# Split in-projection weights written to DRAM by the first token block and read back by the other two

## The chip, the cores and the metric

The kernel runs on one core of one Trainium2 chip. The metric is device time in microseconds of one execution. Below, PE is the matmul engine (TensorE) and PEld its weight loads, DVE is VectorE, ACT ScalarE, POOL GpSimd, and SP the engine whose queue issues all of this kernel's DMAs.

## The reference, cut to what matters

One layer of a hybrid encoder: a projection, a gated MLP mixer beside a Mamba-2 state-space mixer, an output projection, a layer norm, and a squared-ReLU feed-forward. The change touches the projection alone.

```python
def mixer(x, ssm_state, conv_state, offset, w_in, ...):
    proj = jnp.einsum('bld,de->ble', x, w_in)          # 1024 -> 4624 columns
    u, v, z, xbc, dt = ...                             # slices of proj
    y_g, v_rows = gmlp_mix(u, v, ...)
    xbc, new_conv = causal_conv(xbc, conv_state, conv_w, conv_b)
    y, new_ssm = ssd_scan(xs, dtp, a, bm, cm, ssm_state)
    y_s = gated_rms_norm(y, z, ssd_norm_g)
    out = jnp.einsum('ble,ed->bld', jnp.concatenate([y_g, y_s], axis=-1), w_out)
```

There are 2048 prompt rows and 8 x 16 sample rows, so 17 chunks of 128 rows, all in float32.

## The kernel before, in words

The program has four stages: the mixer (projection, state-space tasks, gated-MLP tasks), the output projection, and the two feed-forward products. Only the mixer is touched; its last projection product runs at about 1085 us of the profiled span.

**Blocks and units.** The 17 chunks are taken in three token blocks of 6, 6 and 5 chunks (`BLOCKS`). Each block walks 18 units of the projection in the order of the list `order` (z0, x4, x5, x0, ... v3); a unit is 256 output columns (272 for z0, which also holds dt). So every unit's weights are used three times, once per block.

**Products in three passes.** A float32 value is split into a high part (rounded to the type fp32r) and a low part (the rest). `split` does this with one cast on ACT (line 55) and one subtraction on DVE (line 56). A product is made from three of the four pairs of parts (`PASSES`), with both parts of both operands in fp32r. `fl_matmul` (line 217, tile `psfl`) serves the x and u units, `tl_matmul` (line 225, tile `pstl`) the z and v units; each unit has 96 to 144 matmuls.

**Weights.** `load_w` allocates a tile `w` for both parts (128 partitions x 2 parts x 8 k-slices x 272) from a pool of two buffers. For each half of k it loads 512 KB of float32 into a staging tile `ws` (the pool `st` of three buffers, shared with `xs_in`, the staging of x) on line 120, and splits it into `w`. At the start of unit i the code asks for the weights of unit i+1, so their buffer is the one that unit i-1 has just left. This is done in every block: 18 x 3 units, two halves each.

**Mixing tasks.** After each unit one task of a list runs: `ssd(b, j, g)`, a state-space task of one chunk and one half of the heads, or `gmlp(b, j)`. An ssd task loads `xs`, `bt`, `bc`, `e` (from `at`) and `z` from DRAM, where the units left them. ACT and DVE turn `e` into decay factors (lines 425 to 432), and PE multiplies them (`yd`, line 439). At the end it writes `ys` (line 504). The buffers of `xs` and `e` are two deep, so a task's loads wait for the task two before it. The gmlp tasks of a block run in the first five units of the next block: they load `v` and `ug` (from `u`) and multiply with `wt` (tile `sg`, line 533).

**What sets the order.** The program is written in the order above, and a scheduler then places each instruction on its engine's list by a timeline of its own. On the chip every engine, SP included, goes through its list in order: an instruction whose wait isn't over holds everything behind it. DMAs take eight semaphores in turn, so the ninth can only be issued when the first has landed.

Of the kernel before, what the change touches and what calls it, by code (L numbers as in the profile page):

```python
# [7 lines left out]
F32 = mybir.dt.float32  # L8
# [6 lines left out]
P = 128  # L15
D = 1024
KD = D // P
# [33 lines left out]
def trunk_kernel(ctx: ExitStack, tc: tile.TileContext, A, O):  # L51
# [30 lines left out]

    right = ExitStack()
    tail = mixer_heads(tc, right, psA, A, O, dr, small, stage, ident, select, rsqrt, split, yg_d, ys_d)
    sums = Sums(nc, A, dr, stage, x1_d)
    out_proj(tc, right, psA, tail, A, dr, small, stage, rsqrt, split, yg_d, ys_d, x1_d, sums.during_out_proj)
# [4 lines left out]
def mixer_heads(ctx, tc, right, psA, A, O, dr, small, sp, ident, select, rsqrt, split, yg_d, ys_d):  # L91
    nc = tc.nc
# [14 lines left out]

    order = ["z0", "x4", "x5", "x0", "x1", "z1", "x2", "x3", "z2", "z3", "u0", "u1", "u2", "u3", "v0", "v1", "v2", "v3"]

    def load_w(u):  # L110
        w = wp.tile([P, 2, KD, 272], F32R, name="w", tag="w")
        for q in range(2):
            load_w_half(w, u, q)
        return w

    def load_w_half(w, u, q):
        n = 272 if u == "z0" else 256
        src = A["w_z0"] if u == "z0" else A["w_in"][[o for o in order if o != "z0"].index(u)]
        s = sp.tile([P, 4, 272], F32, name="ws", tag="st")
        nc.sync.dma_start(s[:, :, :n], src[:, 4 * q:4 * q + 4, :])  # L120
        split(w[:, 0, 4 * q:4 * q + 4, :n], w[:, 1, 4 * q:4 * q + 4, :n], s[:, :, :n])

    def load_x(c0, js):
        for j in js:
            s = sp.tile([P, KD, P], F32, name="xs_in", tag="st")
            nc.sync.dma_start(s, A["xT"][c0 + j])
            split(xw[:, 0, :, j * P:(j + 1) * P], xw[:, 1, :, j * P:(j + 1) * P], s)

    def load_x_half(j, q):
        s = fp.tile([P, 4, P], F32, name="xh_in", tag="f2")  # L130
        k = slice(4 * q, 4 * q + 4)
        nc.sync.dma_start(s, A["xT"][j][:, k])
        split(xw[:, 0, k, j * P:(j + 1) * P], xw[:, 1, k, j * P:(j + 1) * P], s)


    w0 = wp.tile([P, 2, KD, 272], F32R, name="w", tag="w")
# [4 lines left out]
    for j in range(1, BLOCKS[0][1]):  # L141
        for q in range(2):
            load_x_half(j, q)

    def const(name, src, shape):
        t = cl.tile(shape, F32, name=name)
        nc.sync.dma_start(t, src)
        return t
# [51 lines left out]
    def gmlp_constants():  # L200
        nc.sync.dma_start(wt, A["gmlp_wsT"])
        nc.sync.dma_start(cst, A["gmlp_bs"].unsqueeze(0).to_broadcast([P, 8, P]))
        select(wt, [[0, 8], [1, P]], 0, -1)
        for q in range(2):
            rs = psB.tile([P, 4, P], F32, name="rs", tag="b")
            nc.tensor.matmul(rs, ones, wt[:, 4 * q:4 * q + 4, :], start=True, stop=True)
            for i in range(4):
                h = 4 * q + i
                nc.vector.scalar_tensor_tensor(cst[:, h], rs[:, i], lb[:, h:h + 1], cst[:, h], op0=ALU.mult, op1=ALU.add)
        nc.vector.tensor_scalar(cst, cst, 0.5, None, op0=ALU.mult)  # L210
        nc.vector.tensor_scalar(lgh, lg, 0.5, None, op0=ALU.mult)
# [339 lines left out]
    units = [(b, u) for b in range(len(BLOCKS)) for u in order]  # L551
    tasks = []
    nxt = {}

    def run(k):
        for _ in range(k):
            if tasks:
                f, *a = tasks.pop(0)
                f(*a)

    nxt[0] = w0
    for i, (b, u) in enumerate(units):
        c0, n = BLOCKS[b]
        if u == "z0":
            N = n * P
            s = state[b] = {
                "u": dr.tile([P, 8, N], F32, name=f"u{b}"), "v": dr.tile([n, P, D], F32, name=f"v{b}"),
                "z": dr.tile([n, P, D], F32, name=f"z{b}"), "xs": dr.tile([n, P, D + 256], F32, name=f"xs{b}"),
                "bc": dr.tile([P, 2, 2, N], F32, name=f"bc{b}"), "at": dr.tile([n * NH, P], F32, name=f"at{b}"),
                "dt": cl.tile([P, 6, NH], F32, name=f"dt{b}", tag="dt", bufs=2),  # L570
                "vst": cp.tile([P, 6, 4, 6], F32, name=f"vst{b}", tag="vst", bufs=2),
            }
            for k in ("da", "acum", "ea", "dw", "bd"):
                s[k] = cl.tile([P, 6 * NH], F32, name=f"{k}{b}", tag=k, bufs=1 if k == "da" else 2)
        if i + 1 < len(units):
            nxt[i + 1] = load_w(units[i + 1][1])
        w = nxt.pop(i)
        {"x": unit_x, "z": unit_z, "v": unit_v, "u": unit_u}[u[0]](b, w, int(u[1]))
        if u == "v3" and b + 1 < len(BLOCKS):
            load_x(BLOCKS[b + 1][0], range(BLOCKS[b + 1][1]))  # L580
        if u == "z0":
            decays(b)
        if (b, u) == (0, "x5"):
            gmlp_constants()
        if u == "z1":
            tasks += [(ssd, b, j, 0) for j in range(n)]
        if u == "z3":
            tasks += [(ssd, b, j, 1) for j in range(n)]
        if u == "v3":
            tasks += [(gmlp, b, j) for j in range(n)]  # L590
            if b == len(BLOCKS) - 1:
                break
        run(1)
# [535 lines left out]
```

## Time and profile before

| | |
|---|---|
| three runs | 2878.36 us median (2877.48 to 2885.31) |
| the profiled execution | 2879.43 us, its span 2877.7 us |
| PE busy in the span | 2764.5 us (96%) |
| DVE, ACT, POOL busy | 1980.8 (69%), 1171.7 (41%), 383.3 us (13%) |
| blocks of the mixer | first to 383.6 us, second to 757.4 us, third to about 1085 us |
| DMA | 607.31 MB, mean 211 GB/s |

Busy time is an engine's own time in instructions; its waits are not in it. The span is the time from the first to the last instruction of that one execution; the 1.7 us between it and the execution's time lie outside.

### The profile page before, as it was taken

The numbers are of one execution on the slowest core, as the hardware profiler recorded it, in microseconds if no ns is written. First come the engines' busy times: TensorE is split into PE (matmuls) and PEld (weight loads), VectorE is DVE, ScalarE is ACT, GpSimd is POOL, SyncE is SP. The second block draws the span as 40 slices with busy tenths as digits, with TensorE's granted clock in tenths as the row PEclk, the third lists the DMA queues.
The fourth block names the chain that finished last, engine by engine and source line by source line (L and its number), as shares of the span: only waits on it lengthen the run. The fifth ranks groups of instructions, "written<-read, shape, count | busy, mean of one in ns | idle before, by whom it ended". The sixth has DMA issues, their size and how long they took to land.

```text
span 2877.7 us, 42483 instructions
## 1 busy us (share of the span) xinstructions
PE 2764.5 (96%) x15876; PEld 2553.6 (89%) x15876; DVE 1980.8 (69%) x3202; ACT 1171.7 (41%) x2119; POOL 383.3 (13%) x492
## 2 busy tenths in 40 slices
PE   9999999999999999978997999999999999999997
PEld 8998999999999997867877999999999888888886
DVE  6787878877788677555549877666776344544786
ACT  5444434445344443001114556555655333333331
POOL 1232313322234213100000000000000000000011
PEclk9999999999999999999998999999999999999998
DMA  6475566554666548776669988767887455545762
GB/s 197 140 211 192 169 210 196 150 184 158 197 201 171 170 147 251 256 220 223 212 214 321 337 289 294 248 237 260 310 256 239 154 177 176 177 154 180 254 204 107
DMA packets 393151, 607.31 MB, mean 211 GB/s; under 512 B 73568, under 2 KB 283888, under 8 KB 386800
## 3 DMA queue, kind: packets, MB, share of 16 engines
q1 hardware_dynamic: 392944, 604.60, 64.7%
q8 instruction: 124, 2.03, 0.3%
q14 instruction: 83, 0.68, 0.1%
HBM read 410.99 MB, written 193.51 MB: 210 GB/s over the span
## 4 chain that ended last, share of the span: by engine, by line
PE 64%; DMA 14%; DVE 14%; issue 3%; ACT 2%; POOL 1%; SPq 1%; DVEq 0%; ACTq 0%; POOLq 0%
PE pf L876 20%; PE pf L1043 19%; PE psfl L217 7%; PE pstl L225 7%; PE po L678 6%; DMA e<-at 2%; DVE w L56 2%; DMA w2r<-in_w_ff 2%; PE yd L439 1%; DVE acc L294 1%; PE pf L1010 1%; DMA mys<-ys 1%; DMA wos<-in_w_out 1%; DMA xts<-x 1%; DVE og L541 1%
## 5 line engine op out<-in xcount | busy, mean ns | idle before, releaser
L876 PE MATMUL pf<-xt,w 128*128 128x384 f32 (+1 forms) x4032 | 676.8, 330 | 25.6 <-ACT w L55 12.3
L876 PEld LDWEIGHTS pf<-xt,w 128*128 128x128 f32 x4032 | 674.4, 189 | 28.2 <-ACT w L55 13.4
L1043 PE MATMUL pf<-w,ht 128*128 128x512 f32 x2688 | 618.4, 389 | 0.6 <-ACT ht L55 0.6
L1043 PEld LDWEIGHTS pf<-w,ht 128*128 128x128 f32 x2688 | 504.4, 188 | 105.6 <-ACT ht L55 1.1
L217 PE MATMUL psfl<-xw,w 128*128 128x384 f32 (+1 forms) x2880 | 497.4, 330 | 0.0
L217 PEld LDWEIGHTS psfl<-xw,w 128*128 128x128 f32 x2880 | 478.7, 189 | 7.4 <-issue 5.0
L225 PE MATMUL pstl<-w,xw 128*128 128x256 f32 (+1 forms) x3264 | 401.4, 283 | 6.7 <-ACT w L55 6.6
L225 PEld LDWEIGHTS pstl<-w,xw 128*128 128x128 f32 x3264 | 396.3, 190 | 9.9 <-ACT w L55 6.6
L678 PE MATMUL po<-wout,mx 128*128 128x512 f32 x1632 | 379.2, 394 | 26.5 <-ACT mx L55 25.8
L678 PEld LDWEIGHTS po<-wout,mx 128*128 128x128 f32 x1632 | 309.1, 190 | 93.2 <-ACT mx L55 26.8
L56 DVE TENSOR_TENSOR ht<-hr,ht 128x1536 fp32r<-128x1536 f32 (+1 forms) x84 | 132.6, 1579 | 203.6 <-ACT ht L55 201.1
L76 POOL TENSOR_SCALAR lrs<-lmv 128x1 f32<-128x1 f32 x34 | 25.8, 758 | 1668.5 <-DVE lmv L605 1668.3
L55 ACT CAST ht<-hr 128x1536 fp32r<-128x1536 f32 (+1 forms) x84 | 112.3, 1337 | 238.3 <-PE pf L1043 229.7
L55 ACT CAST w<-w2r 128x512 fp32r<-128x512 f32 x176 | 102.1, 618 | 144.3 <-PE pf L1043 95.4
L56 DVE TENSOR_TENSOR w<-w2r,w 128x512 fp32r<-128x512 f32 x176 | 114.8, 687 | 62.4 <-ACT w L55 62.2
L56 DVE TENSOR_TENSOR w<-w1s,w 128x512 fp32r<-128x512 f32 x192 | 132.0, 691 | 31.2 <-ACT w L55 27.5
L56 DVE TENSOR_TENSOR w<-ws,w 128x1024 fp32r<-128x1024 f32 (+1 forms) x108 | 147.6, 1393 | 5.9 <-ACT w L55 5.9
L55 ACT CAST w<-w1s 128x512 fp32r<-128x512 f32 x192 | 117.9, 617 | 76.8 <-PE pf L876 58.4
L55 ACT CAST w<-w1r 128x512 fp32r<-128x512 f32 x144 | 89.1, 619 | 102.5 <-PE pf L876 99.7
L56 DVE TENSOR_TENSOR w<-w1r,w 128x512 fp32r<-128x512 f32 x144 | 99.4, 690 | 25.9 <-ACT w L55 22.9
L294 DVE SCALAR_TENSOR_TENSOR acc<-raw,cw,acc 128x640 f32<-128x640 f32 (+1 forms) x108 | 106.0, 982 | 13.4 <-ACT acc L288 12.6
L55 ACT CAST mx<-mxs 128x512 fp32r<-128x512 f32 x34 | 19.4, 618 | 226.9 <-DMA mxs<-yg 218.1
(220 smaller groups left out, 3091.1 us busy)
## 6 DMA issues: line engine op xcount, KB each, us to landing
ws<-in_w_in SPq DMA_DIRECT2D x102, 512.0 KB, 5.3
w1r<-in_w_ff SPq DMA_DIRECT2D x96, 512.0 KB, 6.4
w1s<-w1s SPq DMA_DIRECT2D x48, 1024.0 KB, 7.6
hr<-hv SPq DMA_DIRECT2D x56, 768.0 KB, 4.6
w2r<-in_w_ff SPq DMA_DIRECT2D x64, 512.0 KB, 4.3
hv<-hs SPq DMA_DIRECT2D x32, 768.0 KB, 6.4
e<-at SPq DMA_DIRECT2D x34, 512.0 KB, 6.6
x<-x SPq DMA_DIRECT2D x33, 512.0 KB, 4.9
```

Source lines behind the costliest of these rows:

```text
L55: nc.scalar.copy(hi, src)
L56: nc.vector.tensor_sub(lo, src, hi.bitcast(F32))
L76: nc.gpsimd.tensor_scalar(out, var, scale, eps, op0=ALU.mult, op1=ALU.add)
L217: nc.tensor.matmul(ps[:, :n], w[:, a, k, f * P:(f + 1) * P], xw[:, b, k, o:o + n], start=(q, i, k) == KORDER[0], stop=(q, i, k) == KORDER[-1])
L225: nc.tensor.matmul(ps[:, :n], xw[:, a, k, j * P:(j + 1) * P], w[:, b, k, :n], start=(q, i, k) == KORDER[0], stop=(q, i, k) == KORDER[-1])
L294: nc.vector.scalar_tensor_tensor(aa, raw[:, k:k + npr], cw[:, ft, k:k + 1], aa, op0=ALU.mult, op1=ALU.add)
L439: nc.tensor.matmul(yd[:, h * HD:(h + 1) * HD], e[:, h], xdt[:, h * HD:(h + 1) * HD], start=True, stop=True)
L541: nc.vector.scalar_tensor_tensor(oo, i0, lgh[:, h:h + 1], k, op0=ALU.mult, op1=ALU.add)
L678: nc.tensor.matmul(acc[c][d], m[c][k // 4][:, a, k % 4], W[q][:, w, i, d * 512:(d + 1) * 512], start=k == 0 and (a, w) == (0, 0), stop=k = ...
L876: nc.tensor.matmul(o, W[i][:, u, k], X[i][:, v, k, :n], start=q + k == 0 and not more, stop=q == 2 and k == 3, skip_group_check=True)
L1010: nc.tensor.matmul(ps[d], h[:, u, k, f], w[d][:, v], start=k + f + q == 0, stop=(k, f, q) == (n - 1, 1, 2))
L1043: nc.tensor.matmul(acc[l], h[:, u, m, j * P:(j + 1) * P], w[m][:, v], start=kg + q + m == 0, stop=(kg, q, m) == (3, 2, 3))
```

## The change

In the first block, `load_w` splits the weights as before and then copies the finished tile `w`, both parts, into a DRAM tile of the unit (`keep_parts`). In the second and third block it loads both parts from there straight into `w`: no staging tile, no cast, no subtraction. The first unit's weights, which are loaded ahead of `load_w`, get the same copy after the loads of x.

```diff
+    parts = {}
+
+    def load_w(b, u):
+
         w = wp.tile([P, 2, KD, 272], F32R, name="w", tag="w")
+        n = 272 if u == "z0" else 256
+        if b > 0:
+            nc.sync.dma_start(w[:, :, :, :n].bitcast(F32), parts[u])
+            return w
         for q in range(2):
             load_w_half(w, u, q)
+        keep_parts(u, w)
         return w
+
+    def keep_parts(u, w):
+        n = 272 if u == "z0" else 256
+        parts[u] = dr.tile([P, 2, KD, n], F32, name=f"w_{u}")
+        nc.sync.dma_start(parts[u], w[:, :, :, :n].bitcast(F32))
...
     for j in range(1, BLOCKS[0][1]):
         for q in range(2):
             load_x_half(j, q)
+    keep_parts("z0", w0)
...
-            nxt[i + 1] = load_w(units[i + 1][1])
+            nxt[i + 1] = load_w(*units[i + 1])
```

Over the program this takes away 72 casts on ACT, 72 subtractions on DVE and 72 loads of 512 KB. It adds 18 writes and 36 loads of both parts, 2048 KB each (2176 KB for z0). The changed file's lines lie 13 or 14 further down (line 120 becomes 133, 415 becomes 429).

The scheduler's lists change with it, up to the end of the mixer; from there on they are the same. First, SP's list at the start of the program, where `w_z_209` is the new DRAM copy of z0. Before:

```order
L147 DMA av<-in_a_log 128x16 [waits DMAHW7_49]
L147 DMA dsk<-in_d_skip 128x16 [waits DMAHW0_49]
L132 DMA xh_in<-in_xT 128x512 [waits DMAHW1_49,DVE_49]
L147 DMA lg<-in_gmlp_ln_gT 128x8 [waits DMAHW2_49]
L132 DMA xh_in<-in_xT 128x512 [waits DMAHW3_49,DVE_49]
```

And of the change:

```order
L161 DMA av<-in_a_log 128x16 [waits DMAHW7_49]
L127 DMA w_z_209<-w 128x4352 [waits DMAHW0_49,DVE_49]
L145 DMA xh_in<-in_xT 128x512 [waits DMAHW1_49,DVE_49]
L161 DMA dsk<-in_d_skip 128x16 [waits DMAHW2_49]
L145 DMA xh_in<-in_xT 128x512 [waits DMAHW3_49,DVE_49]
```

The copy of z0 now stands ahead of the last three loads of x of the first block (two are in these rows) and of the first loads of the next unit's weights.

Second, SP's list in the third block, from one ssd task's `ys` to the next task's, in the u units. Before:

```order
L504 DMA ys_109<-xs 128x512 [waits DVE_49]
L413 DMA bc<-bc_8619 128x2x128 [waits DMAHW3_49,PE_49,Activation_49]
L408 DMA xs<-xs_8618 128x512 [waits DMAHW4_49,DMAHW2_49]
L120 DMA ws<-in_w_in 128x4x256 [waits DMAHW5_49,DVE_49]
L120 DMA ws<-in_w_in 128x4x256 [waits DMAHW6_49,DVE_49]
L243 DMA u_8615<-uo 128x2x640 [waits DMAHW7_49,DVE_49]
L415 DMA e<-at_8620 128x1024 [waits DMAHW0_49,PE_49]
L411 DMA bt<-xs_8618 128x128 [waits DMAHW1_49,DVE_49]
```

And of the change, where `w_u_2720` is the DRAM copy of a u unit's parts:

```order
L518 DMA ys_109<-xs 128x512 [waits DMAHW6_49,DVE_49]
L422 DMA xs<-xs_8521 128x512 [waits DMAHW7_49,DMAHW6_49]
L117 DMA w<-w_u_2720 128x16x256 [waits PE_49]
L427 DMA bc<-bc_8522 128x2x128 [waits DMAHW1_49,PE_49,Activation_49]
L257 DMA u_8518<-uo 128x2x640 [waits DMAHW2_49,DVE_49]
L429 DMA e<-at_8523 128x1024 [waits DMAHW3_49,PE_49]
L425 DMA bt<-xs_8521 128x128 [waits DMAHW4_49,DVE_49]
```

The two staged loads, which waited for DVE to leave a staging buffer, have become one load that waits for PE to leave the buffer of `w`; it stands in the same place, ahead of `u` and `e`.

Third, PE's list at the end of the first block (`x107` is a run of 107 equal matmuls; 272 columns is the next block's z0). Before:

```order
L225 MATMUL pstl<-w,xw 128x256 x37
L439 MATMUL yd<-xdt,e 128x64 x8
L395 MATMUL st<-xw_hi,sm 128x512
...
L395 MATMUL yo<-h_hi,sm 128x512
L225 MATMUL pstl<-w,xw 128x256 x107
L533 MATMUL sg<-wt_4432,v 128x128 x4
L225 MATMUL pstl<-w,xw 128x272 x144
```

And of the change:

```order
L239 MATMUL pstl<-w,xw 128x256 x77
L453 MATMUL yd<-xdt,e 128x64 x8
L239 MATMUL pstl<-w,xw 128x256 x5
L409 MATMUL st<-xw_hi,sm 128x512
L409 MATMUL yo<-h_hi,sm 128x512
L239 MATMUL pstl<-w,xw 128x272 x17
...
L239 MATMUL pstl<-w,xw 128x272 x77
L547 MATMUL sg<-wt_4461,v 128x128 x4
L239 MATMUL pstl<-w,xw 128x272 x42
```

The first block's last ssd task stood 107 matmuls ahead of the block's end and now crosses it; its first `yd` stands 24 matmuls later than before, and those between up to 260 later. In the second block the tasks' `yd` stand within 11 matmuls of where they stood; in the third, one stands 34 earlier and the others within 7.

## Rows read from the trace of the kernel before

**Rows 1.** The page, busy time of each engine.

```profile
PE 2764.5 (96%) x15876; PEld 2553.6 (89%) x15876; DVE 1980.8 (69%) x3202; ACT 1171.7 (41%) x2119; POOL 383.3 (13%) x492
```

**Rows 2.** Windows by block: length, busy PE, PEld, DVE, ACT, POOL, clock, DMA, GB/s.

```profile
8.00:383.60 375.60, 368.12 (x2466) 353.41 (x2467) 296.64 (x539) 186.27 (x392) 94.00 (x154) 1.00 0.59 183
383.60:757.40 373.80, 364.07 (x2520) 358.55 (x2518) 296.64 (x523) 169.24 (x361) 112.77 (x121) 0.99 0.57 177
757.40:1048.00 290.60, 276.84 (x1951) 270.00 (x1951) 225.51 (x412) 129.15 (x283) 94.66 (x99) 0.96 0.58 179
```

**Rows 3.** Waits of PE, 0 to 1130 us: total, times, longest.

```profile
PE yd L439 <- DVE e L432: 14.8, 9, 3.3
PE sg L533 <- DVE v L522: 9.3, 4, 3.5
```

**Rows 4.** Timeline of PE, second and third block: start, length, wait before it.

```profile
555.10 3.65 PE L439 MATMUL yd<-xdt,e 128*128 128x64 f32 x16 [3.30 <-DVE e L432]
...
594.78 5.66 PE L217 MATMUL psfl<-xw,w 128*128 128x384 f32 x31
...
614.92 5.82 PE L217 MATMUL psfl<-xw,w 128*128 128x384 f32 x32
...
888.50 2.69 PE L439 MATMUL yd<-xdt,e 128*128 128x64 f32 x16 [1.74 <-DVE e L432]
...
1025.04 2.69 PE L439 MATMUL yd<-xdt,e 128*128 128x64 f32 x16 [2.11 <-DVE e L432]
```

**Rows 5.** Groups by form, 0 to 1200 us: the weights' subtractions and casts.

```profile
L56 DVE TENSOR_TENSOR w<-ws,w 128x1024 fp32r<-128x1024 f32 x102 | 139.6, 1395 | 4.3 <-ACT w L55 4.2
L55 ACT CAST w<-ws 128x1024 fp32r<-128x1024 f32 x102 | 101.9, 1048 | 6.7 <-DMA ws<-in_w_in 6.6
```

**Rows 6.** Timeline of ACT ahead of the wait at 888.50 us.

```profile
884.68 1.99 ACT L55 CAST w<-ws 128x1024 fp32r<-128x1024 f32 x2
886.57 0.63 ACT L431 ACTIVATE e<-e 128x512 f32<-128x512 f32 x1
```

**Rows 7.** Timeline of SP's queue (start, length of issue), third block, u units.

```profile
967.29 0.32 SPq L408 DMA_DIRECT2D xs<-xs  x1
968.73 1.52 SPq L120 DMA_DIRECT2D ws<-in_w_in  x2
970.34 0.46 SPq L243 DMA_DIRECT2D u<-uo  x1
970.89 0.42 SPq L415 DMA_DIRECT2D e<-at  x1
```

**Rows 8.** Chain that ended last, 528 to 562 and 962 to 982 us: start, length.

```profile
535.33 3.98 DVE w L56 x2
...
539.79 6.49 DMA e<-at
...
970.89 8.61 DMA e<-at
```

**Rows 9.** DMA queues (MB, share) and issues (size, median us to landing).

```profile
q1 hardware_dynamic: 392944, 604.60, 64.7%
...
ws<-in_w_in SPq DMA_DIRECT2D x102, 512.0 KB, 5.3
...
w1s<-w1s SPq DMA_DIRECT2D x48, 1024.0 KB, 7.6
...
ys<-xs SPq DMA_DIRECT2D x34, 256.0 KB, 2.0
```

**Rows 10.** Timeline of ACT at the start: first cast of the second unit's weights.

```profile
20.94 1.05 ACT L55 CAST w<-ws 128x1024 fp32r<-128x1024 f32 x1 [2.82 <-DMA ws<-in_w_in]
```

**Rows 11.** Windows of 10 us at the start and 50 us in gated-MLP stretches, as rows 2.

```profile
20.00:30.00 10.00, 10.00 (x76) 10.00 (x75) 5.39 (x13) 4.63 (x8) 1.09 (x1) 1.00 0.88 302
...
40.00:50.00 10.00, 10.00 (x63) 9.64 (x62) 7.38 (x17) 5.38 (x12) 0.78 (x4) 1.00 0.06 17
...
400.00:450.00 50.00, 45.08 (x283) 43.78 (x282) 37.94 (x84) 21.19 (x44) 13.89 (x18) 0.99 0.74 233
...
800.00:850.00 50.00, 46.10 (x325) 45.57 (x324) 42.02 (x72) 22.25 (x48) 16.90 (x20) 0.97 0.74 233
```

More of the change, by code (lines that the diff above doesn't have):

```diff
@@ L108, in mixer_heads @@
     order = ["z0", "x4", "x5", "x0", "x1", "z1", "x2", "x3", "z2", "z3", "u0", "u1", "u2", "u3", "v0", "v1", "v2", "v3"]
-    def load_w(u):
+    parts = {}
+    def load_w(b, u):
         w = wp.tile([P, 2, KD, 272], F32R, name="w", tag="w")
+        n = 272 if u == "z0" else 256
+        if b > 0:
+            nc.sync.dma_start(w[:, :, :, :n].bitcast(F32), parts[u])
+            return w
         for q in range(2):
             load_w_half(w, u, q)
+        keep_parts(u, w)
         return w
+    def keep_parts(u, w):
+        n = 272 if u == "z0" else 256
+        parts[u] = dr.tile([P, 2, KD, n], F32, name=f"w_{u}")
+        nc.sync.dma_start(parts[u], w[:, :, :, :n].bitcast(F32))
     def load_w_half(w, u, q):
```

## The prediction

> **What bounds the kernel now.** I read the page's busy times first: PE is busy for 96% of the span, DVE for 69%, ACT for 41% [rows 1]. The change takes work from DVE and ACT and gives it to the DMA queue, so it can only win where PE waits for one of these two, and it loses where PE waits for a transfer. The windows by block say how much there is to win [rows 2]. In the second and third block, the only ones that lose work on DVE, PE is idle for 373.8 - 364.1 = 9.7 us and 290.6 - 276.8 = 13.8 us. Beside that its clock, which is granted at 2.4 or 1.2 GHz, had a mean of 0.99 and 0.96 of full speed; time at a mean clock c loses 1 - c of it, so 3.7 and 11.6 us. All that can be won there is about 39 us, 1.3% of the time. The waits of PE then say what it waited for [rows 3]: the mixing product `yd` waited nine times for DVE's last step on `e`, 14.8 us in all, and the gated-MLP product four times for DVE's `v`, 9.3 us. Seven of the nine, 12.7 us together, lie between 533 and 1026 us, the longest and the last among these rows [rows 4]. In the u units of the second block PE doesn't wait at all: its units follow each other at 614.92 - 594.78 = 20.1 us [rows 4], the sum of its own work.
>
> **What is removed.** A weights' subtraction takes 1.395 us of DVE, a cast 1.048 us of ACT [rows 5]. 72 of each go, 100 us of DVE and 75 us of ACT, 2.8 and 2.1 us per unit of the last two blocks. PE doesn't see most of it: DVE was busy 79% of the second block (296.6 of 373.8 us) and needs not be faster where PE is never late. It counts in three kinds of places on the way to `yd`.
> - Two casts stand between ACT's two exponentials of `e` and hold the second for 1.99 us [rows 6]; the 1.74 us that PE then waits at 888.50 us [rows 4] is that.
> - SP's list holds `e` behind the staged loads, and the second of these can't be issued before DVE has split an older half: before the 3.30 us wait at 555.10 us, DVE's two splits of 3.98 us lead straight to the load of `e` [rows 8].
> - In the third block the same happens each unit. The two staged loads are issued from 968.73 us on, then `u`, and `e` at 970.89 us [rows 7], which lands 8.61 us later [rows 8]; that load is on the chain for most of a unit.
>
> If all seven waits went, with the half-speed stretches near them, this would win 12.7 us and most of the 3.7 + 11.6 us: 28 us. If what takes the splits' place on SP's list is as late, it wins nothing. I take 16 us, since four of the seven waits (555, 888 and the two last) have a split in their way as the rows show it, and those are the longer ones.
>
> **What is added.** A transfer of both parts is 2048 KB. Its price has two sides.
>
> Its share of the DMA engines: 604.6 MB took 64.7% of 2877.7 us [rows 9], so 3.1 us per MB, and 2.1 MB take 6.5 us of all sixteen engines. In the first block 18 writes are 117 us; its DMA share goes from 0.59 to 0.59 + 117/375.6 = 0.90. In the other two a unit's 1 MB becomes 2.1 MB, 3.2 us more, 36 times: 0.57 becomes about 0.75 [rows 2]. Neither is full.
>
> Its time to landing: 512 KB took 5.3 us and 1024 KB 7.6 us in their own traffic [rows 9], so 2.3 us for each further 512 KB and 12.2 us for 2048 KB; the least is the 6.5 us of the engines with the 2.0 us that 256 KB needed [rows 9], 8.5 us. I take 12. The work that hides it is the unit in between: the load waits for PE to leave the buffer of `w`, and PE comes back to that buffer a unit later, 20.1 us in the second block, about 18 us in the third. So 6 to 8 us are left; before, the split was over some 5 us after the buffer was free. If SP comes to the load more than 6 us late, because an instruction ahead of it on the list still waits, each further us is one of PE.
>
> Behind the waiting load on SP stand `bc`, the write of `u` and `e`. In the third block `e` is issued about 2.3 us earlier, since its neighbours no longer wait for the splits, but has 3.2 us more in front of it in the queue, of which about 1 us starts earlier because the load needs no staging buffer. The two cancel within 1 us, and what is left is the relief on DVE and ACT: hence not the whole 28 us.
>
> The Trainium skill, "DMA: Bandwidth & Descriptors", section "Queues, rings and completion order", says that each DMA engine takes the descriptors of a ring in order, and all of this kernel's loads come from SP. That is the rule that speaks against this change: what PE waits for stands behind what nobody waits for. By it alone `e` would land later by the whole added megabyte, and the gain would turn into the slower rival below. The same page's section "Anatomy of one DMA" puts a transfer at about 2.0 us and its bytes over 436 GB/s; an estimate from it for 2048 KB is 6.8 us. By that the load would keep 11 us of cover, and the sum would stay as it is.
>
> Four places cost something.
> - **The start.** The copy of z0 stands ahead of the last loads of x and of the next unit's weights. DMA is busy at 0.88 from 20 to 30 us [rows 11], and ACT's first cast of those weights at 20.94 us had waited 2.82 us for them [rows 10]. 6.5 us more moves it to 27.4 us, and PE wants them at about 28 us with the split still to come. Between nothing and 6.5 us; I take 3. It can't be more, since the DMA share is 0.06 from 40 to 50 us [rows 11].
> - **The rest of the first block** at a share of 0.90. Products need their weights a unit ahead and the order now puts the mixing tasks behind up to 260 further products, so later landings of `xs`, `e` and the decode states needn't stop PE. Nothing to 15 us; I take 4.
> - **The gated-MLP stretches** at the start of the second and third block: DMA share 0.74, PE idle 4.9 and 3.9 us of 50 [rows 11]. One more MB per unit of some 18 us adds 0.18, to 0.92. The loads of `v` and `ug` that stand behind the weights come 3.2 us later, DVE is freer by 2.8 us. -3 to +12 us; I take 4.
> - **The u and v units of the second block**: PE sets the pace and has 20 us of cover: 0.
>
> Later stages keep their order and start earlier or later with the mixer. The sum is -16 + 3 + 4 + 4 = -5 us against the profiled 2879.4 us: 2874.4. The median of the three runs lies 1.1 us below that execution, so 2873.3; I say 2874.
>
> **The rivals.**
> - *Clearly faster* (2860 us): the relief counts in full, -26 us, and the first block costs 3 to 7 us in all. For it: the clock of the third block comes back only if its waits go as a group. Against it: `e` is still the late one in the u units, and its queue has not become shorter.
> - *Slower, the queue* (2900 us): `e`, `v` and `xs` land behind 2 MB transfers. In the third block ten mixing tasks come 2 us later, 20 us, less the 6 us that ACT and DVE give back; the first block costs 7. It decides as soon as `e` takes more than about 10 us to land after its issue in the third block, against 8.6 now. The share of 0.75 there speaks against it, the 8.6 us for 512 KB that alone would need some 5 for it.
> - *Nothing to see*: PE is the bound and hides both sides, 2878 us. The skill's "Perfetto Trace Analysis", section "Identifying the Most-Contended Engine", says to improve the busiest engine; DVE at 69% isn't it [rows 1]. This case and my forecast lie within 0.3% of each other.
>
> **How the numbers follow.** A change under about 0.3% (8.6 us) can't be told from none here. Chances: 0.40 for within 0.3%, which holds my sum and the last rival; 0.33 for the faster case; 0.27 for the slower one. The bounds add to -28 + 0 + 0 - 3 = -31 and 0 + 6.5 + 15 + 12 = +33 us; the range leaves out a tenth at either end: 2855 to 2902. The likeliest case's own range is 2870 to 2882.
>
> **What would show it.** Right: no waits of `yd` for DVE above 1.5 us in the third block, a clock there of 0.98 or more, the load of `w` landing in 9 to 13 us and never named as what PE waits for; first block's DMA share near 0.9 and some 3 us more until the second unit ends. Wrong: PE's weight loads waiting for a DMA of `w` (the cover is gone), `e` taking over 10 us in the third block, or new waits of PE in the first block for `xs`, `h` or `e` of more than 10 us together.

## The result, and the profile after

The changed kernel takes 2861.28 us (median of five, 2857.08 to 2870.22) against 2878.36 us (median of five, 2875.51 to 2885.31): a ratio of 0.9944, 95% interval 0.9925 to 0.9962, so 0.56% faster. The profiled execution of after is the fastest of its five, 2857.08 us, 22.3 us below the profiled one of before. The medians are 17.1 us apart, so some 5 us of what the two traces show is scatter between executions.

The page of after, busy times and DMA (queue: packets, MB, share; issues: size, median us to landing), answers to [rows 1, 9]:

```profile
PE 2754.8 (97%) x15876; PEld 2546.6 (89%) x15876; DVE 1891.3 (66%) x3130; ACT 1109.1 (39%) x2047; POOL 358.4 (13%) x492
...
q1 hardware_dynamic: 462160, 680.36, 72.9%
...
w<-w_x SPq DMA_DIRECT2D x12, 2048.0 KB, 10.1
ws<-in_w_in SPq DMA_DIRECT2D x34, 512.0 KB, 7.2
e<-at SPq DMA_DIRECT2D x34, 512.0 KB, 7.0
w<-w_u SPq DMA_DIRECT2D x8, 2048.0 KB, 9.8
```

DVE lost 89.5 us and ACT 62.6 us; PE's own busy time fell by 9.7 us, although it does the same 15876 matmuls. Most of that is the clock: its mean rose from 0.983 to 0.985 of full speed, some 6 us of the span. Windows by block, columns as in [rows 2]:

```profile
8.00:391.60 383.60, 373.33 (x2454) 357.74 (x2455) 289.05 (x523) 184.35 (x387) 100.07 (x145) 0.98 0.86 277
391.60:761.50 369.90, 362.37 (x2528) 357.49 (x2527) 256.68 (x501) 138.76 (x326) 101.97 (x131) 1.00 0.74 235
761.50:1034.50 273.00, 266.65 (x1952) 261.86 (x1951) 186.00 (x379) 100.90 (x251) 76.58 (x99) 0.99 0.80 253
```

Against [rows 2] the first block is 8.0 us longer, the second 3.9 us shorter, the third 17.6 us shorter. Read each with its idle time and its clock: in the third block PE is idle for 273.0 - 266.65 = 6.4 us in place of 13.8, and the granted clock is 0.99 in place of 0.96, which is 0.03 x 280 = 8 us. These two make 15 to 16 of the 17.6. In the first block the sign is the other way: idle 10.3 us in place of 7.5, and clock 0.98 in place of 1.00, some 6 to 8 us.

Waits of PE, 0 to 1130 us, answers to [rows 3]:

```profile
PE yd L453 <- DVE e L446: 4.8, 4, 1.9
PE sg L547 <- DVE v L536: 4.2, 5, 1.7
PE yo L483 <- DMA h<-in_state_ssm: 3.1, 2, 2.5
PE yd L453 <- POOL xdt L448: 2.6, 4, 1.0
PE st L485 <- ACT x L476: 2.6, 2, 1.8
```

The two waits for DVE fell from 24.1 us together to 9.0. No wait names the load of `w`; the only wait for `w`, 6.6 us for ACT's first cast at the start, is in both kernels. Of the waits of the first block those for `h` and `xdt` were there before (3.8 and 1.7 us, the latter partly in the second block); that for `x` is new. Of the four waits of `yd` two are left above 1.5 us in the third block, one in its last u unit and one in its first v unit (timeline of PE, answers to [rows 4]):

```profile
992.65 1.97 PE L453 MATMUL yd<-xdt,e 128*128 128x64 f32 x16 [1.57 <-DVE e L446]
...
1011.53 2.51 PE L453 MATMUL yd<-xdt,e 128*128 128x64 f32 x16 [1.87 <-DVE e L446]
```

Where the time goes is best read from the start of each unit on PE (the first `pstl` or `psfl` of a unit in the timeline). After minus before: second unit +0.3 us, second block's start +8.0, its x1 unit (when all of the first block's mixing and all but one of its gated-MLP tasks are done) +12.2, its u0 unit +4.1, third block's start +4.2, its x1 unit -0.8, its last v unit -13.5, the output projection's first product -15.8, its last -23.6, last product -23.5. The first block's loss comes late: at its u0 unit the changed kernel is 5.7 us ahead, since its mixing tasks stand later on PE's list, and at the second block's x5 unit it is 17.3 us behind.

### The profile page after: what moved, and what is told of

Its sections match the earlier page's. It is cut to its first block, busy times and chain, and to the rows that moved or that the text cites. A ratio compares the mean times of both kernels' runs of the same rounds, so it can differ in the third digit from the quotient of the medians.

```text
span 2854.4 us, 42311 instructions
## 1 busy us (share of the span) xinstructions
PE 2754.8 (97%) x15876; PEld 2546.6 (89%) x15876; DVE 1891.3 (66%) x3130; ACT 1109.1 (39%) x2047; POOL 358.4 (13%) x492
## 4 chain that ended last, share of the span: by engine, by line
PE 69%; DMA 15%; DVE 8%; ACT 2%; issue 2%; SPq 2%; POOL 1%; DVEq 0%; ACTq 0%; POOLq 0%
PE pf L1057 21%; PE pf L890 21%; PE psfl L231 9%; PE pstl L239 8%; PE po L692 6%; DMA e<-at 3%; PE pf L1024 2%; PE yd L453 1%; DMA w2r<-in_w_ff 1%; DMA xts<-x 1%; DMA mys<-ys 1%; DMA v<-vo 1%; DMA wos<-in_w_out 1%; DMA tv<-w2r 1%; DMA out_ssm_sample<-h 1%
## 5 line engine op out<-in xcount | busy, mean ns | idle before, releaser
L239 PE MATMUL pstl<-w,xw 128*128 128x256 f32 (+1 forms) x3264 | 413.0, 287 | 6.7 <-ACT w L55 6.6
L239 PEld LDWEIGHTS pstl<-w,xw 128*128 128x128 f32 x3264 | 402.5, 192 | 15.3 <-ACT w L55 6.6
L308 DVE SCALAR_TENSOR_TENSOR acc<-raw,cw,acc 128x640 f32<-128x640 f32 (+1 forms) x108 | 108.4, 1004 | 12.2 <-ACT acc L302 11.4
L247 ACT ACTIVATE gt<-gt 128x256 f32<-128x256 f32 (+1 forms) x116 | 52.4, 452 | 92.1 <-DVE gt L246 92.0
## 6 DMA issues: line engine op xcount, KB each, us to landing
w<-w_x SPq DMA_DIRECT2D x12, 2048.0 KB, 10.1
```

The source lines that it names most:

```text
L239: nc.tensor.matmul(ps[:, :n], xw[:, a, k, j * P:(j + 1) * P], w[:, b, k, :n], start=(q, i, k) == KORDER[0], stop=(q, i, k) == KORDER[-1])
L247: nc.scalar.activation(t[:, :n], t[:, :n], AF.Tanh, scale=GK * GC)
L308: nc.vector.scalar_tensor_tensor(aa, raw[:, k:k + npr], cw[:, ft, k:k + 1], aa, op0=ALU.mult, op1=ALU.add)
```

## The experiments

Below, A is the time from the first product to the x1 unit of the second block, B from there to the third block's start, C from there to the output projection's first product, D that projection's length, all in us of the profiled execution. The ratio is to the kernel before, run beside each.

| kernel | median | ratio, 95% | A | B | C | D |
|---|---|---|---|---|---|---|
| before | 2878.4 | 1 | 462.9 | 287.9 | 331.5 | 413.6 |
| after | 2861.3 | 0.9944 (0.9925-0.9962) | 475.1 | 279.8 | 311.5 | 405.9 |
| e1 copies only | 2884.4 | 1.0025 (1.0012-1.0039) | 475.7 | 287.4 | 330.5 | 409.7 |
| e8 three writes | 2850.0 | 0.9913 (0.9892-0.9934) | 457.7 | 285.7 | 311.9 | 408.8 |
| e4 second writes | 2869.6 | 0.9977 (0.9964-0.9990) | 464.9 | 295.8 | 316.1 | 410.3 |
| e9 staging used | 2867.0 | 0.9967 (0.9955-0.9980) | 472.7 | 280.8 | 319.5 | 406.6 |
| e10 v split | 2858.5 | 0.9938 (0.9922-0.9954) | 467.9 | 280.9 | 314.7 | 412.4 |
| e12 z, x copied | 2867.8 | 0.9973 (0.9963-0.9983) | 465.8 | 285.7 | 318.6 | 412.4 |
| e5 casts stay | 2868.0 | 0.9971 (0.9960-0.9983) | 468.4 | 285.7 | 316.9 | 408.3 |
| e6 subtractions stay | 2908.3 | 1.0106 (1.0087-1.0125) | 477.4 | 301.8 | 334.3 | 410.2 |
| e11 GpSimd writes | 2858.6 | 0.9936 (0.9915-0.9958) | 470.1 | 280.5 | 315.5 | 407.0 |
| e16 low only | 2875.9 | 0.9996 (0.9984-1.0007) | 471.6 | 288.1 | 322.1 | 409.4 |
| e19 two writes | 2855.3 | 0.9924 (0.9903-0.9945) | 469.5 | 279.9 | 310.8 | 405.9 |
| e13 GpSimd, v split | 2860.2 | 0.9946 (0.9928-0.9964) | 470.3 | 281.1 | 313.8 | 409.2 |

Behind A to D stands one execution of each kernel. Five of them (after, e1, e5, e6, e9) have the same first block, and their A lies between 468.4 and 477.4 us; four (after, e8, e11, e19) have the same third block, and their C lies between 310.8 and 315.5. A difference in A under some 9 us, or in C under some 5, shows nothing by itself.

**e1: the copies alone.** Blocks 2 and 3 go on loading and splitting.

```diff
-        if b > 0:
-            nc.sync.dma_start(w[:, :, :, :n].bitcast(F32), parts[u])
-            return w
...
-        keep_parts(u, w)
+        if b == 0:
+            keep_parts(u, w)
```

> The first block writes its 18 copies of 2 MB, but blocks 2 and 3 load and split the weights as before, so nobody reads the copies. Theory 1 (the gain of the change is the work that DVE and ACT lose in blocks 2 and 3, the price is the writes): the start of the third x unit of block 2 comes about 12 us later than before, as it does in the changed kernel, nothing is won behind it, and the time is 2878 + 12 = 2890 us. Theory 2 (the writes cost nothing by themselves; block 1 is slower in the changed kernel because the loads of block 2 come earlier on the same list): 2878 us within 4.

A grew by 12.8 us, as in the changed kernel (12.2), and C stayed at 330.5 us. The median is 0.25% above before, less than the 12 us expected, 7.6 us. Theory 1 holds for the place of gain and price. Windows by block of e1:

```profile
8.00:393.80 385.80, 372.71 (x2454) 355.79 (x2455) 289.56 (x522) 186.78 (x387) 97.63 (x146) 0.99 0.85 273
393.80:769.80 376.00, 367.87 (x2532) 361.89 (x2530) 303.08 (x540) 171.56 (x364) 121.42 (x130) 0.98 0.59 180
769.80:1060.00 290.20, 274.70 (x1947) 268.11 (x1946) 224.62 (x410) 128.81 (x283) 93.02 (x99) 0.96 0.59 178
```

The third row is that of [rows 2]: 15.5 us idle, clock 0.96. Only where the splits leave does this block get shorter.

**e8: the loads nearly alone.**

```diff
         if b > 0:
-            nc.sync.dma_start(w[:, :, :, :n].bitcast(F32), parts[u])
+            src = parts["z0" if u == "z0" else ("x4", "x5")[order.index(u) % 2]]
+            nc.sync.dma_start(w[:, :, :, :n].bitcast(F32), src)
...
-        keep_parts(u, w)
+        if u in ("x4", "x5"):
+            keep_parts(u, w)
```

> Only three copies are written (z0, x4, x5), and all units of blocks 2 and 3 read these three in turn, so that the products of most units there have another unit's weights; sizes, loads and their number are those of the changed kernel, 15 writes of 2 MB are gone. Theory 1 (the writes are the price): block 1 and the first gated-MLP stretch lose little against before, 0 to 3 us in place of 12, and the time is 2861 - 10 = 2851 us. Theory 2 (the price of block 1 is one of order, not of bytes): 2861 us within 4.

2850 us, about a microsecond from theory 1. Its windows by block:

```profile
8.00:382.70 374.70, 367.52 (x2465) 352.77 (x2466) 291.48 (x538) 184.53 (x390) 96.58 (x155) 1.00 0.64 204
382.70:749.80 367.10, 361.92 (x2519) 357.37 (x2518) 248.72 (x485) 137.15 (x323) 101.16 (x121) 0.99 0.73 232
749.80:1022.00 272.20, 265.31 (x1944) 260.86 (x1943) 185.04 (x377) 100.72 (x251) 76.69 (x99) 0.99 0.80 252
```

The first block has its clock of 1.00 back and is as short as before; the third is as short as after. So the reading side is worth about 27 us of the median (2876.7 - 2850.0), and the other 15 writes cost 9 to 11, by the ratios or by the medians of this kernel and the changed one. Theory 2 isn't excluded by this run, though. In e8 PE takes up the first block's mixing tasks exactly where it did before, and those of the other blocks exactly where the changed kernel does (counted by the products of the projection ahead of each `yd`): with the writes, the later place of the first block's mixing went too. The price of 9 to 11 us is that of both together.

**e4: the second block writes.**

```diff
-        if b > 0:
+        if b > 1:
...
-        keep_parts(u, w)
+        if b == 1:
+            keep_parts(u, w)
...
-    keep_parts("z0", w0)
```

> Block 2 splits as before and writes the copies, only block 3 reads them. Theory 1 (relief in blocks 2 and 3, price by the writes wherever they stand): block 1 is as before; block 2 loses the 8 us and the 5 us that it had won and pays up to 12 us for the writes; block 3 wins its 13 us and what follows it: 2878 + 0 to 12 - 13 - 10 = 2855 to 2867 us. Theory 3 (the gain behind block 3, of some 10 us, comes from staging buffers that are free for the output projection's loads): the same, since they are free here too. If block 2 hides the writes (its share of the DMA engines goes from 0.57 to about 0.88), this version is as fast as the changed kernel or faster.

2869.6 us, just past the upper end: B is 295.8 us, 7.9 more than before, so the second block doesn't hide the writes; its v units alone, from v0 to the third block, took 89.7 us in place of 82.1. The price is not that of the first block's start or decode states alone. Here too the writes come with a later place of the mixing: the second block's `yd` stand up to 95 products of the projection later than before.

**e5 and e6: one part of the split stays.** Both versions stage the raw weights again and load one part of 1 MB.

```diff
-            nc.sync.dma_start(w[:, :, :, :n].bitcast(F32), parts[u])
+            nc.sync.dma_start(w[:, 1, :, :n].bitcast(F32), parts[u][:, 1])
+            for q in range(2):
+                s = stage_half(u, q)
+                nc.scalar.copy(w[:, 0, 4 * q:4 * q + 4, :n], s[:, :, :n])
```

`stage_half`, not shown here, loads half of the raw weights into a staging tile. e6 loads part 0 and subtracts instead:

```diff
-            nc.sync.dma_start(w[:, :, :, :n].bitcast(F32), parts[u])
+            nc.sync.dma_start(w[:, 0, :, :n].bitcast(F32), parts[u][:, 0])
...
+                nc.vector.tensor_sub(w[:, 1, k, :n], s[:, :, :n], w[:, 0, k, :n].bitcast(F32))
```

> Block 1 writes both parts as in the changed kernel. In blocks 2 and 3 the low part comes from DRAM and the high part is still cast by ACT from the two staged loads, so that only DVE's subtractions are gone. Theory D (the relief is DVE's: its splits held the staging buffers and so SP's list): nearly all of the gain of blocks 2 and 3 stays, 2861 to 2866 us. Theory A (it is ACT's: casts between the exponentials): the 20 us of block 3 are not won, 2880 us or more with the price of block 1.

> The other way round: the high part comes from DRAM, the low part is still subtracted by DVE from the staged loads, so that only ACT's casts are gone. Theory D: 2880 us or more, block 3 as long as before (331 us from its first unit to the first product of the output projection, 312 in the changed kernel). Theory A: 2861 to 2866 us, block 3 near 312 us. If both halves win half, each of the two versions shows a block 3 near 321 us.

With the casts kept (e5) C is 316.9 us: 14.6 of the 20.0 us are won without touching them. e5's time, 2868 us, is 2 us above the range of theory D, with a B of 285.7 us in place of 279.8; in the third block theory D holds. With the subtractions kept (e6) C is 334.3 us, nothing is won, and the time is 1.1% above before. What the casts alone are worth e6 can't say, since its subtraction has a new wait. DVE on tile `w`, 391 to 1040 us of e6 (what ended its idle time, us, times):

```profile
  DMA w<-w_u: 15.1, 6
  DMA w<-w_x: 12.8, 8
```

DVE goes through its list in order, so these 27.9 us stand in front of the steps that PE waits for: waits of PE in e6, 391 us to the output projection:

```profile
PE yd L464 <- DVE e L457: 16.7, 12, 4.1
PE pstl L250 <- DVE vo L259: 4.5, 4, 1.7
```

The changed kernel has 4.8 us for `e` there and no wait for `vo`. In these two kernels, then, a load of weights was harmless where only PE needs it a unit later, and dear where DVE must touch what it brings.

**e9: the staging buffers stay in use in the third block.**

```diff
...
+            if b == 2:
...
+                for q in range(2):
+                    s = sp.tile([P, 4, 272], F32, name="ws", tag="st")
+                    nc.sync.dma_start(s[:, :, :n], src[:, 4 * q:4 * q + 4, :])
+                    nc.gpsimd.tensor_copy(kept[:, q], s[:, 3, n - 1:n])
```

> The changed kernel, but each unit of block 3 also loads its raw weights into two staging buffers as before, and GpSimd reads one column of each; the splits stay away. Theory 1 (the gain behind block 3 has to do with DVE and ACT, which are ahead): 2861 us, or a few us more for the 17 further MB. Theory 3 (it comes from staging buffers that are free for the output projection's loads): the output projection's first product starts no earlier against the last v unit than before and its stretch is as long as before, so 8 to 10 us are lost again: 2870 us.

D stayed at 406.6 us and the step from the last v unit to the first product at 15.6 us (after 15.3, before 17.6): theory 3 gets no support. But on SP's list the staged loads had moved far ahead, and the output projection's first loads stood at the u0 unit of the third block: the buffers were not held where it matters, and the run doesn't refute it either. The 5.7 us that it lost lie in C, with 18 MB more on the queue, a read by GpSimd, and the third block's mixing tasks up to 229 products later on PE's list.

**e10 and e12: fewer copies.** The v units, then the u units too, load and split in all three blocks (`if b > 0 and u[0] != "v"`; `if b > 0 and u[0] in "zx"`, and the same for `keep_parts`).

> The v units' weights are neither copied nor loaded as parts: all three blocks load and split them, the other 14 units go as in the changed kernel. Theory 1a (the copies of the second half of block 1 are what costs; the four of the v units move the mixing of that block behind its end): the stretch from the first v unit of block 1 to the x4 unit of block 2, 122.5 us in the changed kernel and 105.9 before, comes down to about 110; block 3 pays 3 us for its v splits; the time is 2861 - 12 + 3 = 2852 us. Theory 1b (each of the 18 copies costs its share, some 0.7 us): 2861 - 3 + 3 = 2861 us.

> Only the z and x units are copied and read back; u and v units load and split in all three blocks. Theory 1a: against the version that splits v alone, block 1 gives back the 2 to 3 us of the u copies, and block 3 loses the relief in its u units, 3 to 5 us (from u0 to v0 there it was 76.4 us before and 71.6 after): 2852 + 1 to 3 = 2854 us. Theory 1b: 2861 - 6 + 7 = 2862 us.

From v0 of the first block to x4 of the second e10 needs 112.3 us, near the 110 of theory 1a, but the units before are slower, and A falls by 7.2 us against after, in e12 by 9.3, which is hardly more than A scatters. Behind it C is +3.2 and +7.1 us, D +6.5 us in both. e10 lies between theories 1a and 1b and can't be told from the changed kernel; e12 is above both, some 6 us slower.

**e16: half the bytes.** `parts[u]` holds the low part alone; blocks 2 and 3 are those of e5.

```diff
-        parts[u] = dr.tile([P, 2, KD, n], F32, name=f"w_{u}")
+        parts[u] = dr.tile([P, KD, n], F32, name=f"w_{u}")
-        nc.sync.dma_start(parts[u], w[:, :, :, :n].bitcast(F32))
+        nc.sync.dma_start(parts[u], w[:, 1, :, :n].bitcast(F32))
```

> Only the low parts are kept: block 1 writes 1 MB per unit, blocks 2 and 3 load the low part from DRAM and stage and cast the high part, as in the version whose casts stay (2868 us), which reads the same bytes and whose block 1 writes 2 MB per unit. Theory 1 (the bytes of the copies, and the later place of the mixing tasks that comes with them, are the price of block 1): the order of the products in block 1 is nearly that of before, the stretch from the first product to the x1 unit of block 2 falls from 468 to about 460 us, and the time to 2860 us. If the price hangs on the number of copies and not on their size: 2868 us within 3.

A miss: A is 471.6 us with half the bytes, e5 has 468.4, and theory 1 wanted about 8 us less than e5. Here PE takes up the first block's mixing nearly where it stood before (the decode products `yo` lie behind 764 to 1520 of the projection's products; before 747 to 1490, after 793 to 1719), and it waits early, for the decode states, in place of late. Waits of PE in e16, 7 to 385 us:

```profile
PE yo L493 <- DMA h<-in_state_ssm: 6.6, 6, 2.9
PE yd L463 <- POOL xdt L458: 3.7, 1, 3.7
```

C is 5 us longer than in e5 with the same work there, and the median 8 us; what makes this difference stays open.

**e11, e19, e13: queue and number of writes.** e11 issues the copies from GpSimd, e19 writes each part by its own transfer, e13 is e11 with e10's rule for v.

```diff
-        nc.sync.dma_start(parts[u], w[:, :, :, :n].bitcast(F32))
+        nc.gpsimd.dma_start(parts[u], w[:, :, :, :n].bitcast(F32))
```

```diff
+        for a in range(2):
+            nc.sync.dma_start(parts[u][:, a], w[:, a, :, :n].bitcast(F32))
```

> The changed kernel with the 18 copies issued by GpSimd on its own queue in place of SP's list. Theory Q (block 1 pays because a copy stands on SP's list, waits there for its split, and holds the loads behind it): block 1 and the first gated-MLP stretch fall from 475 to about 465 us, the time to 2851 us. Theory 1 (it pays for the bytes of the copies, whose share of the DMA engines is the same from either queue, and for the later place of the mixing tasks that comes with them): 2861 us within 4; GpSimd's own work waiting behind the copies would make it slower than that.

> The changed kernel with each copy written by two transfers of 1 MB, high part and low part, in place of one of 2 MB: 36 writes, the same bytes. Theory N (block 1 pays about 1 us for each write, whatever its size: from its first product to the x1 unit of block 2 it took 463 us with no copy, 466 with 10, 468 with 14, 472 with 18 of either size): that stretch grows from 475 to about 490 us, the time to 2875 us. Theory M (it pays for late landings of what the mixing of block 1 loads, which depend on the bytes in the queues and on where the mixing stands, not on the number of writes): 2861 us within 5.

> Two edits that were each 2 to 3 us below the changed kernel, together: the copies go from GpSimd's queue, and the v units are split in all three blocks and not copied. If their gains are real and add: 2855 us, with block 1 and the first gated-MLP stretch at about 465 us in place of 475. If they are the scatter of a time by its order: 2861 us within 4.

e11 and e13 are the changed kernel's time within the intervals: theory Q falls as far as its 10 us go, and the two small gains don't add. e19 refutes theory N: with 36 writes A is 469.5 us, 5.6 less than with 18, where the theory wanted 15 more. Its first block and second block:

```profile
8.00:379.50 371.50, 367.34 (x2452) 352.05 (x2453) 289.16 (x521) 182.80 (x385) 94.82 (x146) 1.00 0.87 286
379.50:755.90 376.40, 366.28 (x2531) 361.50 (x2530) 256.51 (x502) 139.28 (x327) 103.62 (x130) 0.98 0.73 230
```

The DMA share of the first block is as high as in the changed kernel (0.87, 0.86), yet its clock is 1.00 and it is 12.1 us shorter; the second block then loses 6.5 us of that. So neither the bytes (e16), nor the number of writes (e19), nor SP's list (e11) sets the price of the copies by itself. With all units copied A lay between 468 and 477 us in eight kernels, with 10 or 14 of them at 466 to 470, with three or none at 458 to 465. Only the last group lies clear of the scatter. What is shown is that the price comes with the copies. Some inputs of the mixing land later with them (medians between 7 and 400 us: `e` 7.6 us after its issue in place of 5.9, `z` 7.9 in place of 4.8; e8 has 5.7 and 4.9). That how many of these late landings stop PE depends on where the list has the mixing would fit the runs, but isn't shown; which transfer is held by which was not separated.

Apart from e8, whose units have other weights, no version is shown to be faster than the changed kernel; e19, e10 and e11 have lower medians, within the intervals.

## Why the prediction was right and wrong

The measured 2861 us lies in the range (2855 to 2902), but the likeliest case, 2874 and no change that can be told, was not what came. The time is that of the rival *clearly faster* (2860 us). In the order of the sum (-16 + 3 + 4 + 4, and 0 for the later stages) the profiled pair gives: relief -20.8 us, start +0.3, first block with the second block's gated-MLP stretch +11.9, the third block's gated-MLP stretch -5.0, later stages -10.1. So the rival is met in part by luck: its relief of 26 us came, but its price of the first block (3 to 7 us) was too low, and gains in the later stages, which it leaves out, made up for that. One sum of the prediction is slightly off, and nothing hangs on it: the bounds of -31 and +33 us, less a tenth of their 64 us at either end, give 2854 to 2905 around 2878, not 2855 to 2902.

- **The relief on DVE and ACT, -16 us, was too small.** In the profiled pair the rest of the second block, from its x1 to its u0 unit, won 8.1 us, and the rest of the third, from x1 to its last v unit, 12.7: 20.8 us. Windows of these two stretches, before and then after, columns as in [rows 2]:

```profile
469.50:594.80 125.30, 120.50 (x838) 118.35 (x836) 99.72 (x149) 55.41 (x114) 41.65 (x45) 0.97 0.53 152
831.80:1071.20 239.40, 230.38 (x1650) 224.54 (x1649) 183.81 (x316) 111.26 (x245) 72.41 (x76) 0.96 0.53 161
...
481.70:598.90 117.20, 116.83 (x838) 115.61 (x836) 82.87 (x136) 43.91 (x101) 39.07 (x45) 1.00 0.74 218
831.00:1057.80 226.80, 221.94 (x1651) 217.94 (x1651) 155.86 (x294) 87.62 (x216) 58.85 (x75) 0.99 0.74 233
```

  PE's idle time fell from 13.8 to 5.2 us, and what the clock takes, by 1 - c, from 13.3 to 2.3 us. The 16 us are four sevenths of 28: 7.3 us of the waits and 8.7 of the clock. The waits came out near that: of the seven with 12.7 us, 4.8 us are left, in four waits. Which ones went was in part luck. Of the four chosen, those at 555 and 987 us went and that at 888 us is down to 0.18, but that at 1025 us is still 1.87; of the others two went and that at 909 us fell to 1.16 (with 2.56 us the second longest of the seven, so the chosen four were not the longer ones); one of 1.57 us is new. The step that failed is to let the half-speed stretches go in the same proportion as the waits: 11.0 of their 13.3 us went. Of the four waits that are left only the last, at 1011.53 us, has a fall of the clock behind it; from 761.5 us to there the granted clock is 1.00. The two bullets on DVE's splits are borne out by e5; the one on the casts is not shown.
- **The gated-MLP stretches, +4 us, had the wrong sign for one of the two.** Windows of 50 us, columns as in [rows 11], shifted with the units:

```profile
413.00:463.00 50.00, 44.92 (x286) 43.77 (x286) 34.99 (x83) 17.74 (x40) 14.81 (x19) 1.00 0.90 286
804.00:854.00 50.00, 49.48 (x366) 49.26 (x365) 38.96 (x76) 19.22 (x44) 14.55 (x20) 1.00 0.97 311
```

  The share rose to 0.90 and 0.97, as worked out (0.92). In the second block's stretch PE is idle as before, 5.1 us; in the third's 0.5 us in place of 3.9, and from z0 to x1 the third block won 5.0 us. The wait of `sg` for DVE's `v` there fell from 3.5 us to 0.5 at the longest, which fits DVE's 2.8 us per unit weighing more than the later landing. With these 5.0 the relief is 25.8 us, which is the 26 of the rival.
- **The first block, +4 us, cost 12.2** up to the second block's x1 unit (its gated-MLP stretch included, where the other part of that term would lie). It is within the bounds (15), but the term counted only waits, not the clock behind them. One of them in the timeline of PE, and the windows around it:

```profile
158.57 0.50 PE L485 MATMUL st<-x,bm 96*128 96x512 f32 x1 [1.79 <-ACT x L476]
```

```profile
155.00:160.00 5.00, 3.21 (x24) 2.96 (x23) 2.66 (x7) 2.75 (x6) 0.18 (x1) 0.95 1.08 265
160.00:164.00 4.00, 4.00 (x24) 4.00 (x24) 4.00 (x5) 1.89 (x3) 0.00 (x0) 0.64 0.57 173
```

  PE idles for 1.79 us, and then runs at 1.2 GHz for a while: by the clock 0.05 x 5 + 0.36 x 4 = 1.7 us more are lost while it is busy. By the matmuls themselves, which start every 213 ns there in place of 117, it is some 1.5 us. The wait costs nearly twice its length. (A DMA share above 1 comes from counting a transfer whole in the window in which it starts.)
- **The start, +3 us, cost 0.3.** The copy of z0 did move the cast of the next weights (timeline of ACT, answers to [rows 10]), and the DMA share of the windows rose:

```profile
26.75 1.05 ACT L55 CAST w<-ws 128x1024 fp32r<-128x1024 f32 x1 [2.27 <-DMA ws<-in_w_in]
```

```profile
20.00:30.00 10.00, 10.00 (x75) 9.84 (x75) 4.65 (x10) 5.21 (x9) 0.00 (x0) 1.00 0.98 326
40.00:50.00 10.00, 10.00 (x63) 9.64 (x62) 7.69 (x18) 5.27 (x9) 0.67 (x4) 1.00 1.01 315
```

  5.8 us later, near the 6.5 worked out; PE came to it at 27.85 us in place of 27.6. The cast had ended at 27.80 us, so the cover was used up to 0.05 us: that the start cost almost nothing was luck in part.
- **The load of `w`** landed 9.1 to 10.1 us after its issue by the medians of the four kinds of units, 12.6 us at the latest (12 taken). PE never waited for it, and the u units of the second block kept their 20.1 us: right. The estimate of 6.8 us from the Trainium skill, "DMA: Bandwidth & Descriptors", section "Anatomy of one DMA", is below every one of them; the section gives its two terms for transfers that GpSimd issues, and SP issued these. **The queue** did not come: `e` in the third block, ten loads, landing min/median/max, before and after:

```profile
DMA to landing us min/median/max: 4.2/7.5/8.8
```

```profile
DMA to landing us min/median/max: 4.2/7.5/8.9
```

  That the two sides cancel is borne out, but the load ahead left earlier by more than the 1 us that was taken: in the u units the load of `w` was issued 4.1 to 6.3 us ahead of `e`, where the second staged load had been issued 0.5 to 1.0 us ahead of it. The Trainium skill, "DMA: Bandwidth & Descriptors", section "Queues, rings and completion order", has each DMA engine take the descriptors of a ring in order. This is not contradicted by the landings, since the load ahead had left earlier; the price that the prediction worked out by it alone, the whole added megabyte, was wrong here.
- **Later stages, 0 us, was wrong in the trace**: 2.3 us were won up to the output projection's first product, and D is 7.8 us shorter. Two rows, of before and of after:

```profile
1272.33 2.92 PE L678 MATMUL po<-wout,mx 128*128 128x512 f32 x6 [14.65 <-ACT mx L55]
```

```profile
1247.90 2.50 PE L692 MATMUL po<-wout,mx 128*128 128x512 f32 x5 [10.55 <-ACT mx L55]
```

  4.1 us of the 7.8 are this one wait. In e1, whose list is that of before from the second block on, the same wait took 12.70 us, and in the twelve others 9.0 to 12.6: before's trace has the longest, and this part I hold for scatter, as the 5 us by which the profiled pair is wider than the medians suggest. The 2.3 us are the wait for `mx` ahead of the projection's first product, 2.45 us at 1088.84 us in before, and the clock behind it (0.84 over the next 11 us) is 1.8 of the 7.8. This wait is 1.4 to 3.3 us in seven of the eight kernels that split or cast weights in the third block's v units (0.99 in e13), and never above 0.7 in the six others. That staging buffers come free earlier fits this; e9 was meant to show it and didn't hold them, so it is not shown.
- **What would show it.** Clock of the third block 0.99 (0.98 asked), `w` in 9 to 13 us and not waited for, first block's DMA share 0.86: as said. Two waits of `yd` above 1.5 us remained: not as said. The new waits of the first block stayed under the 10 us that were to show the forecast wrong (PE's idle time grew by 2.8 us), and yet the block cost 12: that limit left out the clock.

## What to carry to other kernels

Work taken from an engine that isn't the busiest pays where the busy engine waits for it in line: here 100 us off DVE at 69% and 75 us off ACT at 41% were worth about 27 us, as the version nearly without writes shows. The copies, with the later place of the mixing that comes with them, took 9 to 11 of them back. Price the waits of TensorE at more than their length: in the two stretches above, the half-speed clock took as much as the idle time (13.3 and 13.8 us), and 11.0 us of it went where 8.6 of the idle time did. When spare DMA share is what pays for a change, put the traffic where its consumer comes a unit later: no load that only PE reads was waited for at a share of 0.8, while the load with a DVE step on it (e6) held DVE up for 27.9 us, in a kernel 1.1% slower than before.

## What was not expected of the hardware

- In the third block ten loads of `e` of 512 KB landed in the same 7.5 us (median) at a DMA share of 0.58 and of 0.80.
- The writes of 2 MB landed 8.7 to 10.1 us after their issue from SP (medians by kind of unit) and those of x units 13.2 us after it from GpSimd (9.9 from SP), and the time was the same within the intervals.
- In the first block more was lost by the granted clock (0.98 in place of 1.00, 6 to 8 us) than by the waits themselves (2.8 us more idle time), behind waits of 1.0 to 2.5 us. Not each such wait is followed by a slow stretch: one of 1.86 us at 451 us and one of 1.57 us at 993 us were not.
